# Two fused transformer blocks on one core: three vector products of the modulation moved from the first attention into the recurrence, score products split in three

## The chip, the cores and the metric

The kernel runs on one core of a Trainium2 chip, in one launch. The metric is the device time of one execution in microseconds. TensorE (PE) does the matrix products, VectorE (DVE) and ScalarE (ACT) the elementwise work, GpSimd (POOL) some small vector work and the gathers of expert rows, SyncE (SP) issues most of the transfers. Each engine works through its own list of instructions in order; where one needs another's result, it waits on a semaphore. Matrix products accumulate in PSUM, and all other tiles live in SBUF.

## The reference

Two transformer blocks follow each other on 512 rows of 1024 numbers. The change lies in the first one. Cut to what matters:

```python
def first_block(x, c, ctx, c_ctx, ...):
    mod_x = silu(c) @ w_mod + b_mod                       # 6 parts of 1024
    mod_c = silu(c_ctx) @ w_mod + b_mod
    sh1, sc1, gt1, sh2, sc2, gt2 = split(mod_x, 6)        # parts 0 to 5
    px = split(modulate(rms_norm(x, norm1), sh1, sc1) @ w_in, splits)
    pc = split(modulate(rms_norm(ctx, norm1), csh1, csc1) @ w_in, splits)
    na_x = neighbourhood_attention(q, k, v, k_ctx, v_ctx, na_rpb)   # 8 heads of 64
    hg_x = hgrn2_mixer(px[3:], pc[3:], lb, hg_norm)                 # 4 heads of 128
    x = x + gt1 * (concat([na_x, hg_x]) @ w_out)
    x = x + gt2 * peer_ffn(modulate(rms_norm(x, norm2), sh2, sc2), ...)
    return rms_norm(x, norm_f)
```

`modulate(h, shift, scale)` is `h * (1 + scale) + shift`. Of the modulation, parts 0 and 1 are needed before the projections, part 2 (gt1) behind the output projection, parts 3 and 4 (sh2, sc2) before the expert stage, part 5 (gt2) at the end of the block. In the attention each of 512 queries attends to a window of the grid and to all 256 rows of the context, with a bias for the place in the window.

## The kernel before

The first block runs in this order: modulation parts 0 and 1; the normalised input `hT`, kept in columns; then the recurrence with its projections; then the projections of v, k and q for the attention; the attention; the output projection `w_out`; the routing of the experts; the experts. The order of instructions on each engine is not that of the text: a scheduler takes the program as written and, from its dependencies and from the buffers of the tile pools (a tile of a pool with two buffers must wait until the last but one of the same name has been read), writes an order for each engine.

**Split products.** A product of full precision is made from two tiles in a 32-bit type that PE takes in one pass (`fp32r` in the rows of ACT and DVE): `hi`, a rounded copy made by ACT (L190), and `lo`, the remainder, made by DVE (L191). Three products, hi by hi, hi by lo and lo by hi, add up in PSUM. Every projection is made so: `wload` (L198) loads 256 columns of weights and splits them, `proj_T` and `proj_N` run through eight row tiles with three products each. A plain f32 operand does it in one instruction, which the profile records as two.

**Vector products.** `gemv_T` (L247) makes one part of the modulation, a vector of 1024. The weights come in eight tiles `wg` of 512 KB, two buffers; for each tile `gemv_rows` issues four f32 products that stand beside one another in columns of 32 of the array and add to four groups of rows of one PSUM tile. ACT copies the result into an SBUF tile `row`. Then eight small products with the constant `pick` add the four groups of rows and turn the row into columns of `modT`, with the bias added by DVE. All of one part's columns are made behind its whole row.

**Recurrence** (L385 to L506). Two parts `p`, each of two heads. A part first makes its projections: forget gates in both directions (`F`, from L392), `Qr` (L403), `vn` (L412), `gs` (L421). Then for each head there are a diagonal step and seven levels `k` (from L445): ACT copies halves of the keys into a tile `Kx` (a pool `gla2` with two buffers), PE makes four f32 products of `Kx` and `Q` into a PSUM tile `pA`, DVE merges them and decays keys and queries for the next level. After the levels, PE turns the keys (`kn`), makes the states, the output `pO`, and turns the normalised result `yn` (L506) into a half of `yT`. The scheduler puts the projections of the next part, or those of the attention, between the levels.

**Attention** (L538 to L611). Four pairs of heads `hp2`, each with four blocks of 128 queries. The score products `pS<-kT,qT` are f32 products on 64 rows of the array, one head of the pair on the upper and the other on the lower half: 256 or 384 columns for the window, 256 for the context. DVE adds the bias `nab` and takes the maximum (L578), ACT takes the exponential (L580), PE turns the result (L587), ACT or DVE copies it out (`pT`, L589), PE makes the values `pv`. The bias of a head is loaded once per pair, 2304 columns, in three buffers. Behind pair 0, 1 and 2 the text has `gemv_T` for parts 2, 3 and 4, and the scheduler spreads their products over the pairs behind.

Of the kernel before, what the change touches and what calls it, by code (L numbers as in the profile page):

```python
# [18 lines left out]
P = 128  # L19
# [113 lines left out]
NAB = 3  # L133


def program(tc, a, out, tap=None):
# [41 lines left out]
    class Split:  # L178
        def __init__(self, hi, lo):
            self.hi, self.lo = hi, lo  # L180

# [65 lines left out]
    def gemv_T(pl, ps_pool, wname, part, v, slot, bias, tag="pm"):  # L247
        row = pl.tile([P, D], F32, name="row", bufs=1)
        for h2 in range(2):
# [7 lines left out]
            S.copy(row[:, h2 * 512:(h2 + 1) * 512], ps)  # L257
        ps = ps_pool.tile([P, 512], F32, name=tag)[:, :2 * KT].rearrange("p (k o) -> p k o", o=2)
        for kt in range(KT):
            mm(ps[:, kt, :], row[:, kt * P:(kt + 1) * P], pick[:, v:v + 2])  # L260
        V.tensor_add(modT[:, slot, :], ps[:, :, 0], bias)
# [17 lines left out]

    eY = ExitStack()  # L280
    yp = pool(eY, "yT", side="right")
    yT = yp.tile([P, KT, T], F32, name="yT")
# [85 lines left out]
    kT = kvp.tile([P, 4, TC], F32, name="kT")  # L368
# [14 lines left out]

    with ExitStack() as es:
# [5 lines left out]
        pO = pool(es, "pO", 1, PSUM)  # L390
        for p in range(2):
            Fs = [g2.tile([P, 2, TC], F32, name="F") for _ in range(2)]  # L392
            for d in range(2):
                w = wload("w_in", 8 + 2 * d + p)
                for h in range(2):
# [26 lines left out]
            for t in range(NB):  # L422
# [4 lines left out]
                V.tensor_mul(gs[:, t, :], gs[:, t, :], hgnB)  # L427
            for h in range(2):
# [78 lines left out]
                S.copy(yT[:, 4 + p * 2 + h, :], ps)  # L507
# [16 lines left out]
    def kproj(j):  # L524
        w = wload("w_in", 2 + j)
        for m in range(2):
            ps = pm.tile([P, 512], F32, name="pm")
            proj_T(ps, w, m * P, P, hT, 0, T)
            S.copy(kT[:, 2 * j + m, :T].rearrange("p (b r c) -> p b r c", r=8, c=16), ps.rearrange("p (r b c) -> p b r c", b=4, c=16))
            ps = pm.tile([P, 512], F32, name="pm")  # L530
            proj_T(ps, w, m * P, P, hT, T, L)
            S.copy(kT[:, 2 * j + m, T:], ps[:, :L])
# [5 lines left out]
    with ExitStack() as es:  # L538
        np_ = pool(es, "na")
        n2 = pool(es, "na2", 2)  # L540
        gv = pool(es, "gemv")
        qT = np_.tile([P, 4, T], F32, name="qT")
# [14 lines left out]
        for hp2 in range(4):  # L557
            pv = pV.tile([P, 4, P], F32, name="pv")
            sums = n2.tile([P, 8], F32, name="sums")
            bts = []  # L560
            for hh in range(2):
                bt = n2.tile([P, 2304], F32, name="nab", bufs=NAB)
                DMA.dma_start(bt, a["nab"][2 * hp2 + hh])
                bts.append(bt)
            for qb in (0, 1, 3, 2):
# [3 lines left out]
                b0 = 512 - nw if nk == 3 else 0  # L569
                pss = [pS.tile([P, 1024], F32, name="pS") for _ in range(2)]  # L570
                for c0, c1, x0 in ((b0, b0 + nw, k0 * P), (b0 + nw, b0 + n, T)):
                    for hh in range(2):
                        mm(pss[hh][:, c0:c1], qT[HH[hh], hp2, qb * P:(qb + 1) * P], kT[HH[hh], hp2, x0:x0 + c1 - c0])
                pTs = []
                for hh in range(2):
                    sc = n2.tile([P, 640], F32, name="sc", bufs=4)
                    mx_ = sm.tile([P, 1], F32, name="mx")
                    V.tensor_tensor_reduce(out=sc[:, :n], in0=pss[hh][:, b0:b0 + n], in1=bts[hh][:, off[qb]:off[qb + 1]], scale=1.0, scalar=NEG, op0=OP.add, op1=OP.max, accum_out=mx_)  # L578
# [24 lines left out]
            V.tensor_mul(yT[:, hp2, :].rearrange("p (r b c) -> p b r c", b=4, c=16), pv.rearrange("p b (r c) -> p b r c", c=16),  # L603
# [663 lines left out]
```

## Time and profile before

| | us |
|---|---|
| runs | 2344.86, 2347.52, 2342.06 |
| median of the runs | 2344.86 |
| profiled execution, its own time | 2337.86 |
| span of its profile | 2336.1 |
| PE busy | 2259.9 |
| DVE busy | 1598.4 |
| ACT busy | 980.3 |
| POOL busy | 249.1 |

The busy times are sums over the span; they do not say which engine holds up which stage. The stages that the change touches lie at these places of the span, by the timeline of PE: projections and recurrence of part 0 from 64 us, the level products of part 0 from about 128 us, those of part 1 from about 233 us, the attention from the first score product at 343.6 us to the first product of `w_out` at 467.9 us, the routing from about 521 us.

### The profile page before, as it was taken

The page shows a single profiled execution, that of the slowest core. Times are in us where ns is not written, and L with a number is a line of the kernel's source. Part 1 is how long each engine was busy: PE and PEld are TensorE (multiplying, and loading weights), DVE is VectorE, ACT ScalarE, POOL GpSimd, SP SyncE. Part 2 cuts the span into 40 slices and gives each one's busy share as a digit, 9 for nine tenths or more (in the row PEclk, how much of TensorE's full clock was granted, in tenths as well). Part 3 has the DMA queues.
Part 4 walks back from the last instruction along what each step waited for, and adds up shares of the span by engine and source line. Part 5 has one row for each costly group of instructions (what it writes and reads, how often), then busy time and mean ns, then how long its engine had stood idle before and what let it go on. Part 6 is the DMA issues. An engine that isn't in the chain of part 4 may idle for free. (4 is left out here: it accounts for less than half of the span.)

```text
span 2336.1 us, 34601 instructions
## 1 busy us (share of the span) xinstructions
PE 2259.9 (97%) x13097; PEld 1942.3 (83%) x13097; DVE 1598.4 (68%) x3193; ACT 980.3 (42%) x1828; POOL 249.1 (11%) x159
## 2 busy tenths in 40 slices
PE   7999999998999999999999999999999999989998
PEld 4899986597779999999988888888888786666888
DVE  3674723354359977999689888888898627767344
ACT  4432333333234335877534333333333434446421
POOL 0000000000000000322222222222130000000000
PEclk9999999999999999999999999999999999999999
DMA  7111135625555574999999999999997231120221
GB/s 265 55 57 55 52 118 178 212 101 178 165 196 158 163 258 153 328 320 319 333 360 396 406 347 349 354 362 363 360 380 263 88 103 42 50 86 28 98 92 55
DMA packets 170871, 481.74 MB, mean 206 GB/s; under 512 B 14864, under 2 KB 87952, under 8 KB 153168
## 3 DMA queue, kind: packets, MB, share of 16 engines
q1 hardware_dynamic: 152272, 345.31, 42.7%
q0 software_dynamic: 18432, 134.23, 14.7%
q8 instruction: 103, 1.69, 0.3%
q14 instruction: 64, 0.52, 0.1%
HBM read 431.76 MB, written 46.66 MB: 205 GB/s over the span
## 5 line engine op out<-in xcount | busy, mean ns | idle before, releaser
L191 DVE TENSOR_TENSOR wl<-wr,wh 128x1024 fp32r<-128x1024 f32 (+1 forms) x378 | 456.7, 1211 | 362.3 <-ACT wh L190 359.8
L190 ACT CAST wh<-wr 128x1024 fp32r<-128x1024 f32 (+1 forms) x378 | 394.0, 1043 | 440.4 <-PE pm L176 196.1
L176 PE MATMUL pS<-h2h,wh 128*128 128x384 f32 x1024 | 348.2, 340 | 7.3 <-ACT S L695 7.2
L176 PE MATMUL pS<-h2h,wl 128*128 128x384 f32 x1024 | 346.1, 338 | 0.0
L176 PE MATMUL pS<-h2l,wh 128*128 128x384 f32 x1024 | 345.5, 337 | 0.0
L839 POOL DMA_INDIRECT uv<-in_uv_dram,idx x128 | 225.8, 1764 | 1006.9 <-DVE pacc L846 688.8
L176 PE MATMUL po<-wl,Wh 128*128 128x512 f32 x768 | 299.6, 390 | 1.8 <-DVE wl L191 1.8
L176 PE MATMUL po<-wh,Wl 128*128 128x512 f32 x768 | 299.5, 390 | 0.0
L176 PE MATMUL po<-wh,Wh 128*128 128x512 f32 x768 | 298.9, 389 | 0.0
L176 PEld LDWEIGHTS pS<-h2h,wh 128*128 128x128 f32 x1024 | 193.4, 189 | 11.7 <-ACT S L695 8.7
L176 PEld LDWEIGHTS pS<-h2l,wh 128*128 128x128 f32 x1024 | 193.3, 189 | 2.0 <-issue 0.8
L176 PEld LDWEIGHTS pS<-h2h,wl 128*128 128x128 f32 x1024 | 193.2, 189 | 0.0
L190 ACT CAST Wh<-W 128x384 fp32r<-128x384 f32 x128 | 65.7, 513 | 267.8 <-PE po L176 162.1
L176 PE MATMUL pm<-h2h,wh 128*128 128x512 f32 x432 | 173.5, 402 | 0.2 <-ACT cr L1106 0.2
L176 PE MATMUL pm<-h2h,wl 128*128 128x512 f32 x432 | 171.8, 398 | 0.0
L176 PE MATMUL pm<-h2l,wh 128*128 128x512 f32 x432 | 171.8, 398 | 0.0
L176 PEld LDWEIGHTS po<-wl,Wh 128*128 128x128 f32 x768 | 144.1, 188 | 31.9 <-DVE wl L191 2.6
L176 PEld LDWEIGHTS po<-wh,Wl 128*128 128x128 f32 x768 | 144.1, 188 | 30.3 <-DVE Wl L191 0.3
L176 PEld LDWEIGHTS po<-wh,Wh 128*128 128x128 f32 x768 | 144.2, 188 | 29.2
L846 DVE SCALAR_TENSOR_TENSOR pacc<-uv,dts,pacc 128x1024 f32<-128x1024 f32 x128 | 163.9, 1281 | 1.9
L840 DVE SCALAR_TENSOR_TENSOR pscr<-uv,h 128x1024 f32<-128x1024 f32 x128 | 156.1, 1219 | 1.9 <-DMA uv<-in_uv_dram,idx 0.9
L191 DVE TENSOR_TENSOR Wl<-W,Wh 128x384 fp32r<-128x384 f32 x128 | 70.8, 553 | 47.9 <-ACT Wh L190 47.8
(410 smaller groups left out, 4100.6 us busy)
## 6 DMA issues: line engine op xcount, KB each, us to landing
wr<-in_uT_dram SPq DMA_DIRECT2D x128, 512.0 KB, 6.0
wr<-in_uv_dram SPq DMA_DIRECT2D x128, 512.0 KB, 7.7
gd<-stg SPq DMA_DIRECT2D x12, 2048.0 KB, 12.6
Gt<-gd SPq DMA_DIRECT2D x32, 768.0 KB, 8.4
sd<-S SPq DMA_DIRECT2D x88, 192.0 KB, 3.9
Sr<-sd SPq DMA_DIRECT2D x88, 192.0 KB, 6.8
wr<-in_w_in_dram SPq DMA_DIRECT2D x32, 512.0 KB, 3.6
wg<-in_w_mod_dram SPq DMA_DIRECT2D x32, 512.0 KB, 4.3
```

Of the source, the lines that this page charges most:

```text
L176: PE.matmul(ps, lhs, rhs, start=first, stop=last)
L190: (ehi or S.copy)(hi, src)
L191: (elo or V.tensor_tensor)(lo, src, hi.bitcast(F32), op=OP.subtract)
L839: G.indirect_dma_start(out=uv, out_offset=None, in_=a["uv"], in_offset=bass.IndirectOffsetOnAxis(ap=idx[b][:, j:j + 1], axis=0))
L840: V.scalar_tensor_tensor(scr, uv[:, :D], 1.0, h2g[b], op0=OP.mult, op1=OP.mult, accum_out=dts[b][:, j:j + 1])
L846: V.scalar_tensor_tensor(acc[b], tl[j - j0][:, D:], dts[b][:, j:j + 1], acc[b], op0=OP.mult, op1=OP.add)
```

## The change

**Parts 2, 3 and 4 of the modulation** leave the attention. A generator `gates()` makes them in twelve quarters of 256 columns. One quarter (`gemv_quarters`) is two `wg` tiles with four products each, a copy of the PSUM row by ACT, two products with `pick` and an addition by DVE. The recurrence's text takes a quarter behind each of five pieces of a part's projections, ten in all, and the last two behind the projections of part 1. The weights have a pool of their own with two buffers; the row is a buffer of the recurrence's tile `Kx`.

**The parts that are left in `gemv_T`** (part 5, and those of the second block) are now turned by halves, in a row tile of half the length.

**The score products** are split: `mm3` issues hi by hi, hi by lo and lo by hi, 64 rows each. q is split where it is projected, k for each pair of heads at the pair's start.

**The bias** is loaded per block of queries, at most 640 columns, in six buffers. **`yT`** is two tiles, of which the half for the attention is allotted behind the recurrence.

```diff
-NAB = 3
+NAB = 6
...
+    def mm3(ps, x, y, xi, yi):
+        mm(ps, x.hi[xi], y.hi[yi], True, False)
+        mm(ps, x.hi[xi], y.lo[yi], False, False)
+        mm(ps, x.lo[xi], y.hi[yi], False, True)
...
     def gemv_T(pl, ps_pool, wname, part, v, slot, bias, tag="pm"):
-        row = pl.tile([P, D], F32, name="row", bufs=1)
...
-            S.copy(row[:, h2 * 512:(h2 + 1) * 512], ps)
-        ps = ps_pool.tile([P, 512], F32, name=tag)[:, :2 * KT].rearrange("p (k o) -> p k o", o=2)
-        for kt in range(KT):
-            mm(ps[:, kt, :], row[:, kt * P:(kt + 1) * P], pick[:, v:v + 2])
-        V.tensor_add(modT[:, slot, :], ps[:, :, 0], bias)
+            row = pl.tile([P, 512], F32, name="row", bufs=1)
+            S.copy(row, ps)
+            ps = ps_pool.tile([P, 512], F32, name=tag)[:, :KT].rearrange("p (k o) -> p k o", o=2)
+            for k in range(4):
+                mm(ps[:, k, :], row[:, k * P:(k + 1) * P], pick[:, v:v + 2])
+            V.tensor_add(modT[:, slot, 4 * h2:4 * h2 + 4], ps[:, :, 0], bias[:, 4 * h2:4 * h2 + 4])
...
+    def gemv_quarters(wl, rows, ps_pool, wname, part, v, slot, bias):
+        for hf in range(4):
+            ps = ps_pool.tile([P, 512], F32, name="pm")
+            for k0 in (0, 4):
+                w = wl.tile([P, 4, GW], F32, name="wg", bufs=2)
+                DMA.dma_start(w.rearrange("p k n -> p (k n)"), a[wname][4 * part + hf][:, k0 * GW:(k0 + 4) * GW])
+                gemv_rows(ps[:, :GW], w, k0)
+            row = rows()
+            S.copy(row, ps[:, :GW])
+            ps = ps_pool.tile([P, 512], F32, name="pm")[:, :4].rearrange("p (k o) -> p k o", o=2)
+            for k in range(2):
+                mm(ps[:, k, :], row[:, k * P:(k + 1) * P], pick[:, v:v + 2])
+            V.tensor_add(modT[:, slot, 2 * hf:2 * hf + 2], ps[:, :, 0], bias[:, 2 * hf:2 * hf + 2])
+            yield
...
+    gw = pool(eG, "gw", side="right")
...
+        def gates():
+            for part in (2, 3, 4):
+                yield from gemv_quarters(gw, lambda: g2.tile([P, T], F32, name="Kx")[:, :GW], pm, "w_mod", part, 0, part, bmT[:, part * 8:part * 8 + 8])
+
+        unit = gates()
         for p in range(2):
             Fs = [g2.tile([P, 2, TC], F32, name="F") for _ in range(2)]
             for d in range(2):
...
+                next(unit)
             w = wload("w_in", 6 + p)
...
+            next(unit)
             vn = gp.tile([P, 6, GW], F32, name="vn")
...
+            next(unit)
             hgnB = gp.tile([P, GW], F32, name="hgnB")
...
+            next(unit)
+            if p:
+                for _ in unit:
+                    pass
             for h in range(2):
                 F_, Qr = Fs[h], Qrs[h]
...
-                S.mul(qT[:, 2 * j + m, :].rearrange("p (b r c) -> p b r c", r=8, c=16), ps.rearrange("p (r b c) -> p b r c", b=4, c=16), 0.125)
+                pr = ps.rearrange("p (r b c) -> p b r c", b=4, c=16)
+                q_ = n2.tile([P, 640], F32, name="sc", bufs=4)[:, :T]
+                S.mul(q_.rearrange("p (b r c) -> p b r c", r=8, c=16), pr, 0.125)
+                split(q_, qT.hi[:, 2 * j + m, :], qT.lo[:, 2 * j + m, :])
...
-            bts = []
-            for hh in range(2):
-                bt = n2.tile([P, 2304], F32, name="nab", bufs=NAB)
-                DMA.dma_start(bt, a["nab"][2 * hp2 + hh])
-                bts.append(bt)
+            kT = Split(n2.tile([P, TC], F32R, name="kTh"), n2.tile([P, TC], F32R, name="kTl"))
+            split(k32[:, hp2, :], kT.hi, kT.lo)
             for qb in (0, 1, 3, 2):
...
+                bts = []
+                for hh in range(2):
+                    bt = n2.tile([P, 640], F32, name="nab", bufs=NAB)
+                    DMA.dma_start(bt[:, :n], a["nab"][2 * hp2 + hh][:, off[qb]:off[qb + 1]])
+                    bts.append(bt)
...
-                        mm(pss[hh][:, c0:c1], qT[HH[hh], hp2, qb * P:(qb + 1) * P], kT[HH[hh], hp2, x0:x0 + c1 - c0])
+                        mm3(pss[hh][:, c0:c1], qT, kT, (HH[hh], hp2, slice(qb * P, (qb + 1) * P)), (HH[hh], slice(x0, x0 + c1 - c0)))
...
-            if hp2 < 3:
-                part = 2 + hp2
-                gemv_T(gv, pm, "w_mod", part, 0, part, bmT[:, part * 8:part * 8 + 8])
```

How the orders moved is seen at three places, all on PE. In the rows below a product reads `output<-moving or weight tile, other tile`, then the size of the operand and how many follow one another. Between two levels of the second head of part 0 (`pA<-Q,Kx` are a level's products, `pm<-hTh,wh` and its like a projection), before:

```order
L176 MATMUL pA<-Q,Kx 128x128 x4
L176 MATMUL pm<-hTh,wh 128x512
L176 MATMUL pm<-hTl,wh 128x512
L176 MATMUL pm<-hTh,wl 128x512
...
L176 MATMUL pA<-Q,Kx 128x128 x4
```

and now, with the sixth quarter (`pm<-wg,cvec` its eight products, `pm<-pick,Kx` the two that turn its row) around the last levels:

```order
L176 MATMUL pm<-wg,cvec 32x256 x3
L176 MATMUL pA<-Q,Kx 128x128 x4
L176 MATMUL pm<-wg,cvec 32x256 x5
L543 MATMUL tp<-ident,yn 128x128 x4
L176 MATMUL pA<-Q,Kx 128x128 x12
L176 MATMUL pm<-pick,Kx 128x2 x2
L176 MATMUL pm<-hTh,wh 128x512
L176 MATMUL pm<-hTl,wh 128x512
L176 MATMUL pm<-hTh,wl 128x512
L176 MATMUL pA<-Q,Kx 128x128 x4
```

Eight projection products stood between two levels there; now three levels (x12) follow one another, and the projection goes on behind the two `pick` products. The row that these need is copied by ACT, whose order is now there:

```order
L488 COPY Kx<-K 128x8x32 x2
L488 COPY Kx<-K 128x4x64 x2
L293 COPY Kx<-pm 128x256
L514 COPY kn<-pA 128x512
L515 COPY kn<-pA 128x128
```

The copy of the quarter's row (L293) stands behind the copies of the last level (four blocks of 64), so it comes after them.

At the end of part 1's projections (`pm<-wh,hTh` and its like), PE's order before:

```order
L176 MATMUL pm<-wh,hTh 128x256
L176 MATMUL pm<-wl,hTh 128x256
L176 MATMUL pm<-wh,hTl 128x256
L176 MATMUL pA<-Qr,Kx 128x128 x4
L176 MATMUL pA<-Q,Kx 128x128 x4
```

and now:

```order
L176 MATMUL pm<-wh,hTl 128x256
L176 MATMUL pm<-wg,cvec 32x256 x8
L176 MATMUL pm<-pick,Kx 128x2 x2
L176 MATMUL pm<-wg,cvec 32x256 x8
L176 MATMUL pm<-pick,Kx 128x2 x2
L176 MATMUL pm<-wg,cvec 32x256 x8
L176 MATMUL pm<-pick,Kx 128x2 x2
L176 MATMUL pm<-wh,hTh 128x256
L176 MATMUL pm<-wl,hTh 128x256
L176 MATMUL pm<-wh,hTl 128x256
L176 MATMUL pA<-Qr,Kx 128x128 x4
L176 MATMUL pA<-Q,Kx 128x128 x4
```

Quarters ten to twelve stand in a row, with no other product between them.

In the attention (`pS` scores, `tp` turned probabilities, `pv` values), PE's order before:

```order
L587 MATMUL tp<-ident,sc 128x128 x8
L176 MATMUL pS<-kT,qT 128x384
L176 MATMUL pm<-wg,cvec 32x256 x4
L176 MATMUL pv<-pT,vp 64x128 x8
L176 MATMUL pm<-wg,cvec 32x256 x4
L176 MATMUL pS<-kT,qT 128x256 x5
L176 MATMUL pm<-wg,cvec 32x256 x4
L587 MATMUL tp<-ident,sc 128x128 x5
L176 MATMUL pS<-kT,qT 128x256
```

and now:

```order
L633 MATMUL tp<-ident,sc 128x128 x5
L176 MATMUL pv<-pT,vp 64x128
L176 MATMUL pS<-kTh,qTh 128x384
L176 MATMUL pS<-kTl,qTh 128x384
L176 MATMUL pS<-kTh,qTl 128x384
L176 MATMUL pv<-pT,vp 64x128 x9
L633 MATMUL tp<-ident,sc 128x128 x4
L176 MATMUL pS<-kTl,qTh 128x256
L176 MATMUL pS<-kTh,qTl 128x256
```

The groups of four vector products between the attention's products are gone, and each score product is three, one head's three ahead of the other's. In the whole attention the 64 score products stood in 35 runs, 24 of them alone; the 192 of the change stand in 37 runs.

## Rows read from the trace of the kernel before

**Rows 1.** The page, part 1: busy time of each engine, share of the span, instructions.

```profile
PE 2259.9 (97%) x13097; PEld 1942.3 (83%) x13097; DVE 1598.4 (68%) x3193; ACT 980.3 (42%) x1828; POOL 249.1 (11%) x159
```

**Rows 2.** Stretches: us; busy PE, PEld, DVE, ACT, POOL (instructions); PE clock; DMA share; GB/s.

```profile
64.00:128.00 64.00, 64.00 (x431) 59.28 (x431) 37.85 (x61) 23.85 (x35) 0.00 (x0) 1.00 0.20 66
128.00:204.00 76.00, 74.17 (x485) 66.09 (x484) 59.50 (x108) 27.15 (x71) 2.94 (x2) 1.00 0.13 44
344.00:468.00 124.00, 116.53 (x929) 76.19 (x926) 46.99 (x137) 51.82 (x110) 0.00 (x0) 0.99 0.54 185
```

**Rows 3.** Waits of PE, 64 to 343 us: us in total, times, longest.

```profile
PE tp L506 <- DVE yn L503: 3.4, 4, 1.1
```

**Rows 4.** Waits of PE in the attention.

```profile
PE pm L176 <- DMA wg<-in_w_mod_dram: 3.1, 4, 1.0
PE pS L176 <- DVE mx L578: 2.5, 5, 0.9
```

**Rows 5.** Groups of PE in the attention: busy us, mean ns | idle before, releaser.

```profile
L176 PE MATMUL pS<-kT,qT 64*128 64x256 f32 (+1 forms) x128 | 36.2, 444 | 2.6 <-DVE mx L578 2.5
L176 PE MATMUL pm<-wg,cvec 128*32 128x256 f32 x192 | 15.2, 391 | 3.2 <-DMA wg<-in_w_mod_dram 3.1
```

**Rows 6.** Timeline of PE, 399 to 405 us: start, us with the tail, records.

```profile
399.91 0.70 PE L176 MATMUL pS<-kT,qT 64*128 64x256 f32 x2
400.54 0.64 PE L176 MATMUL pm<-wg,cvec 128*32 128x256 f32 x8
401.11 0.76 PE L587 MATMUL tp<-ident,sc 128*128 128x128 f32 x5
...
402.17 0.91 PE L176 MATMUL pS<-kT,qT 64*128 64x384 f32 x2
403.01 1.95 PE L176 MATMUL pm<-pick,row 128*128 128x2 f32 x16
404.88 0.33 PE L176 MATMUL pv<-pT,vp 128*64 128x128 f32 x2
```

**Rows 7.** Timeline of PE, 360.5 to 362.5 us.

```profile
360.55 1.57 PE L176 MATMUL pS<-kT,qT 64*128 64x256 f32 x8
362.08 0.77 PE L587 MATMUL tp<-ident,sc 128*128 128x128 f32 x5
```

**Rows 8.** Timeline of PE, 290.7 to 291.2 us, a projection's split products.

```profile
290.74 0.28 PE L176 MATMUL pm<-wh,hTh 128*128 128x256 f32 x1
290.86 0.28 PE L176 MATMUL pm<-wl,hTh 128*128 128x256 f32 x1
```

**Rows 9.** Timeline of PE, 381 to 383 us, the first vector products in the attention.

```profile
381.95 1.07 PE L176 MATMUL pm<-wg,cvec 128*32 128x256 f32 x16
382.95 0.43 PE L176 MATMUL pv<-pT,vp 128*64 128x128 f32 x2
```

**Rows 10.** The tile wg, 343 to 480 us: ns of one (min, median, max), first to last.

```profile
L176 PE MATMUL pm<-wg,cvec x192: 379/379/405, 381.9 to 459.2; 128*32 128x256 f32 x192
DMA to landing us min/median/max: 3.1/4.3/6.9
```

**Rows 11.** Groups of ACT, 64 to 343 us.

```profile
L417 ACT COPY vn<-pm 128x256 f32<-128x256 f32 x12 | 4.5, 373 | 24.3 <-PE pm L176 24.3
```

**Rows 12.** Timeline of PE, 159 to 178 us, products of two levels.

```profile
170.00 1.05 PE L176 MATMUL pA<-Q,Kx 128*128 128x128 f32 x8
...
175.66 1.13 PE L176 MATMUL pA<-Q,Kx 128*128 128x128 f32 x8
```

**Rows 13.** Stretches behind the output projection, columns as in rows 2.

```profile
521.00:531.00 10.00, 2.66 (x16) 2.43 (x16) 9.55 (x14) 4.60 (x8) 3.32 (x3) 0.75 0.66 208
531.00:541.00 10.00, 9.28 (x44) 8.51 (x43) 4.81 (x10) 3.35 (x6) 0.00 (x0) 0.73 0.59 211
```

**Rows 14.** Groups of PE's weight loads in the attention.

```profile
L176 PEld LDWEIGHTS pS<-kT,qT 64*128 64x128 f32 x128 | 16.5, 185 | 12.4 <-DVE mx L578 5.6 <-issue 5.2 <-DVE pT L589 0.2
```

**Rows 15.** Waits of PE in the attention up to the first vector product, 343.6 to 381.9 us.

```profile
PE pS L176 <- DVE mx L578: 1.1, 2, 0.8
```

More of the change, by code (lines that the diff above doesn't have):

```diff
@@ L278, in to_hT @@
             split(t[:, :n], x.hi[:, kt, off:off + n], x.lo[:, kt, off:off + n], V.tensor_copy, V.tensor_tensor)
+    def gemv_quarters(wl, rows, ps_pool, wname, part, v, slot, bias):
[12 more added lines that the diff above has]
+            yield
     eY = ExitStack()
-    yp = pool(eY, "yT", side="right")
-    yT = yp.tile([P, KT, T], F32, name="yT")
+    yT = [None] * KT
+    ypb = pool(eY, "yTb", side="right").tile([P, 4, T], F32, name="yTb")
+    for c in range(4):
+        yT[4 + c] = ypb[:, c, :]
     class Turns:
@@ L367, in program @@
     kvp = pool(eH, "nakv")
-    kT = kvp.tile([P, 4, TC], F32, name="kT")
+    k32 = kvp.tile([P, 4, TC], F32, name="kT")
     vp = kvp.tile([P, 6, 512], F32, name="vp")
@@ L382, in program @@
     V.tensor_scalar(lb1, lb0, -1.0, 1.0, op0=OP.mult, op1=OP.add)
+    eG = ExitStack()
+    gw = pool(eG, "gw", side="right")
     with ExitStack() as es:
@@ L506, in program @@
                     PE.transpose(ps[:, c * P:(c + 1) * P], yn[:, c, :], ident)
-                S.copy(yT[:, 4 + p * 2 + h, :], ps)
+                S.copy(yT[4 + p * 2 + h], ps)
+    V.scalar_tensor_tensor(modT[:, 4, :], modT[:, 4, :], 1.0, n2T, op0=OP.add, op1=OP.mult)
+    eG.close()
+    ypa = pool(eY, "yTa", side="right").tile([P, 4, T], F32, name="yTa")
+    for c in range(4):
+        yT[c] = ypa[:, c, :]
     def vproj(j):
@@ L528, in kproj @@
             proj_T(ps, w, m * P, P, hT, 0, T)
-            S.copy(kT[:, 2 * j + m, :T].rearrange("p (b r c) -> p b r c", r=8, c=16), ps.rearrange("p (r b c) -> p b r c", b=4, c=16))
+            S.copy(k32[:, 2 * j + m, :T].rearrange("p (b r c) -> p b r c", r=8, c=16), ps.rearrange("p (r b c) -> p b r c", b=4, c=16))
             ps = pm.tile([P, 512], F32, name="pm")
             proj_T(ps, w, m * P, P, hT, T, L)
-            S.copy(kT[:, 2 * j + m, T:], ps[:, :L])
+            S.copy(k32[:, 2 * j + m, T:], ps[:, :L])
     vproj(0)
@@ L540, in program @@
         n2 = pool(es, "na2", 2)
-        gv = pool(es, "gemv")
-        qT = np_.tile([P, 4, T], F32, name="qT")
+        qT = Split(np_.tile([P, 4, T], F32R, name="qTh"), np_.tile([P, 4, T], F32R, name="qTl"))
         def qproj(j):
@@ L577, in program @@
                     mx_ = sm.tile([P, 1], F32, name="mx")
-                    V.tensor_tensor_reduce(out=sc[:, :n], in0=pss[hh][:, b0:b0 + n], in1=bts[hh][:, off[qb]:off[qb + 1]], scale=1.0, scalar=NEG, op0=OP.add, op1=OP.max, accum_out=mx_)
+                    V.tensor_tensor_reduce(out=sc[:, :n], in0=pss[hh][:, b0:b0 + n], in1=bts[hh][:, :n], scale=1.0, scalar=NEG, op0=OP.add, op1=OP.max, accum_out=mx_)
                     V.tensor_scalar_mul(mx_, mx_, -1.0)
@@ L602, in program @@
             S.copy(rn, rs_)
-            V.tensor_mul(yT[:, hp2, :].rearrange("p (r b c) -> p b r c", b=4, c=16), pv.rearrange("p b (r c) -> p b r c", c=16),
+            V.tensor_mul(yT[hp2].rearrange("p (r b c) -> p b r c", b=4, c=16), pv.rearrange("p b (r c) -> p b r c", c=16),
                          rn.rearrange("p (b r c) -> p b r c", b=4, c=16))
@@ L606, in program @@
                 qproj(1)
-            if hp2 < 3:
-                part = 2 + hp2
-                gemv_T(gv, pm, "w_mod", part, 0, part, bmT[:, part * 8:part * 8 + 8])
-        V.scalar_tensor_tensor(modT[:, 4, :], modT[:, 4, :], 1.0, n2T, op0=OP.add, op1=OP.mult)
-    dbg("yT", yT)
     eH.close()
@@ L663, in program @@
         for kt in range(KT):
-            split(yT[:, kt, :], yS.hi[:, kt, :], yS.lo[:, kt, :], S.copy, V.tensor_tensor)
+            split(yT[kt], yS.hi[:, kt, :], yS.lo[:, kt, :], S.copy, V.tensor_tensor)
         for j in range(4):
```

## The prediction

> **What bounds the kernel now.** The page comes first: TensorE (PE) is busy for 97% of the span [rows 1]. That alone does not say whether a stage could take more work, so the table by stages comes next [rows 2]. While the first recurrence and its projections run (64 to 204 us), PE is busy in 64.0 of 64 us and in 74.2 of 76; in the first attention (344 to 468 us) it is busy in 116.5 of 124. VectorE (DVE) and ScalarE (ACT) are busy there for 47 and 52 us of 124. The waits say the same more sharply: from 64 to 343 us PE waits for another engine only four times, 3.4 us in all [rows 3], and in the attention for 3.1 us on the weights of the vector products and 2.5 us on the softmax [rows 4]. So both stages, the one that loses work and the one that gets it, are bound by PE's own queue. Work that moves from one to the other is worth nothing by itself; what counts is what PE pays around it: changes of array shape, waits, and the clock.
>
> **What leaves the attention.** The page's groups count 192 records of the vector product there [rows 5]; a group of eight records (four products, one beside the other in columns of 32) is one step, so there are 24 steps. In the timeline such a step starts at 400.54 and the next work at 401.11 [rows 6]: 0.57 us, with the drain behind it. 24 x 0.57 = 13.7 us. The sixteen records that turn a row into a column start at 403.01 and end with the next start at 404.88: 1.87 us, three times, 5.6 us. The waits for these weights go too: 3.1 us [rows 4]. Together 22.4 us.
>
> **The score products.** A plain f32 product that stands alone costs 0.63 us at 256 columns (399.91 to 400.54) and 0.84 us at 384 (402.17 to 403.01) [rows 6]; in a run it is cheaper: eight records, so four products, take 1.53 us [rows 7], 0.38 us each. In the order of before, 64 products stand in 35 runs, 24 of them alone: two thirds of the alone ones at 0.63, one third at 0.84, 16.8 us, and 40 at about 0.4, 16 us, so 33 us. The change has 192 products with 64 rows; the trace has none in the split type with 64 rows. The nearest row is the split type with 128 rows: one every 0.12 us at 256 columns [rows 8], 0.18 at 384 in proportion. 144 x 0.12 + 48 x 0.18 = 25.9 us, and 37 runs at about 0.2 us for the change of shape (the 0.63 alone against 0.38 in a run gives that) make 33.3 us: no gain if the two heads never overlap. If they always did, half of 25.9 is saved, 13 us. The order issues the three products of one head before those of the other, which is nearer to the first end: I take 3 us gained. The added splits of k and q on ACT and DVE, under 2 us for each of four head pairs, I cost at nothing: both engines are idle more than half of this stage [rows 2]. The bias table in quarters moves the same bytes. The attention thus gives back 22.4 + 3 = 25.4 us.
>
> **What the recurrence pays.** (a) Twelve quarters. Two adjacent steps cost 1.00 us with the drain (381.95 to 382.95) [rows 9], and four transposing records at 1.87 / 16 another 0.47: 1.5 us x 12 = 18 us, all on the path, since PE has no gap there [rows 3]. (b) In nine of the twelve places the order puts the transposing products right behind the vector product. They need the row, which ACT copies from PSUM after the last product has ended: 0.38 us for that end [rows 10], 0.37 us for a copy of this shape [rows 11], some 0.1 us of hand-over, of which 0.3 was counted as drain. 0.55 x 9 = 5 us. (c) The sixth quarter. Its row is a buffer named Kx, which the level loop of the second head takes in turn; ACT's order has the row's copy behind the last level's copies. The projection cannot go on until that row is transposed, and in PE's order three levels now follow each other with nothing between, where each interval held some eight products before. A level's products start at 170.00, those of the next but one at 175.66 [rows 12]: 2.8 us a level, of which the level's own products take some 0.85. Four intervals lose up to 7.8 us of filling; part returns, since the vector products themselves fill some and levels without filling may follow closer. I take 5 us, bounds 2 and 8. (d) Quarters ten to twelve stand in a row in PE's order, and there are two weight buffers, one quarter's worth. The eleventh's first load can start only when the tenth's first step has freed its buffer: 0.6 us for step and tail, then 4.3 us from issue to landing (3.1 to 6.9) [rows 10], about 5 us a quarter against the 2.05 counted under (a) and (b). Twice 2.95 is 6 us; by the shortest landing 3, by the longest 11. (e) The clock. PE was nearly idle from 521 to 531 (2.7 us busy of 10), and the granted clock was 0.75 and then 0.73 of full speed [rows 13]: PE was at the lower level, 1.2 GHz, for about 0.54 of the second stretch, while it had work for 9.3 us. That lost half of 5.4, 2.7 us. Places (c) and (d) are like it, (c) less so: 1.5 times 2.7 is 4 us, between 0 and 8. The recurrence pays 18 + 5 + 5 + 6 + 4 = 38 us, bounds 26 and 54.
>
> **The other vectors.** The four in the routing stage are now turned by halves, through one PSUM buffer: the second half waits for a turn and an addition. Products stand between; I put a quarter of a microsecond on each, 1 us in all, between 0 and 4.
>
> **The sum.** -25.4 + 38 + 1 = +13.6 us on the profiled execution's 2337.9 us (its span is 2336.1). The runs' median is 2344.9, 7.0 us above it, so I forecast 2344.9 + 13.6 = 2358.5 us, written as 2358.
>
> **Rivals.** *Faster:* the quarters slip into the recurrence without PE standing still. For it speaks that most loads can be issued five or more microseconds ahead. Against it: in (c) and (d) it is the order of PE itself that leaves nothing to do. Then (c), (d) and (e) fall away and 23 us are paid: -25.4 + 23 + 1 = -1.4; with the score products midway between their ends (6.5 us gained) it is -5, 2340 us. It decides once the three cost less than 5 us together. Chance 0.17. *No difference:* stalls of some 10 us and a gain of 27 to 30: within 0.2% of before, 2345 us, chance 0.17. *The attention loses its cover:* the vector products stood where PE would have waited for the softmax. PE waits 2.5 us on it now; without filler the chain of bias, exponential, transposes and copies could show. Against it: until 381.9 us the attention runs without any vector product [rows 10], and PE waits 1.1 us for the softmax there [rows 15]. If half of the 22.4 us comes back as waiting, the sum is +25, 2370 us; chance 0.13. *The split products do not do what they are for:* a weight load that cannot run beside the product before it.
>
> A weight load of a score product takes 185 ns [rows 14], and in the recurrence 128-row products of the split type start every 0.12 us [rows 8] although each has its own load, so loads run beside products there. The Trainium skill, TensorE: Matmul & The Clock Gate, under Part 3: Packing small matmuls, says that a load overlaps with a product in flight only where the two use different groups of rows. The three products of a head use the same rows, so by that rule two loads in each triple would be exposed.
>
> By rows that is 64 x 2 x 0.185 = 23.7 us more: +37, 2382 us. The trace's 128-row products speak against it, so its chance is 0.05. The forecast keeps 0.48.
>
> **How the numbers follow.** The measurement can tell some 0.2%, 4.7 us, from no change. The forecast, the lost cover and the exposed loads are slower by more than that: 0.48 + 0.13 + 0.05 = 0.66. No difference has 0.17 and faster 0.17. The range runs from 2338 (the nearer half of the faster case) to 2374 (the lost cover and a little more); the bounds of (c) to (e) and of the score products lie in it unless they all fall to one side.
>
> **What would show it.** In the changed profile the attention, from the first score product to the first product of the output projection, should last about 99 us instead of 124, without any vector product. The recurrence with its projections should be about 38 us longer. PE should wait for ACT at nine transposing places, by about half a microsecond each; for the weights of the last two quarters by about 3 us each; and stand between the levels of the first part's second head. The granted clock should dip in at least one of these two places. I am wrong if the recurrence grows by less than 28 us, if the attention shrinks by over 35 or by under 15, or if the difference arises behind the first attention.

## The result, and the profile after

The changed kernel takes 2380.69 us (median of 4 runs, 2372.26 to 2383.03); the kernel before takes 2346.19 us beside it (4 runs, 2342.06 to 2350.22). The ratio is 1.0144, interval 1.0121 to 1.0167: 34.5 us slower. The forecast had the sign and 13.6 us; its range ended at 2374 us. The profiled execution has a span of 2377.4 us, 41.3 us more than before, and not 34.5, because the execution profiled before lay 8.3 us under the median of its runs and the one profiled after 1.5 us. The page's first part after (row of before: [rows 1]):

```profile
PE 2281.4 (96%) x13161; PEld 1966.1 (83%) x13161; DVE 1606.0 (68%) x3214; ACT 986.2 (41%) x1842; POOL 259.5 (11%) x159
```

By the timeline of PE, the first score product moved from 343.6 to 393.8 us, the first product of the output projection from 467.9 to 503.2 us. So the recurrence with its projections got 50.2 us longer and the attention 14.9 us shorter: 35.3 of the 41.3 us. The other 6 us lie behind the attention, where one profile cannot tell them: from the first product of the output projection to the end it is 1868.2 us before and 1874.2 after, and in the versions below with the same code there it is anything from 1869.7 to 1875.4. The two stretches as rows (columns as in [rows 2]), before:

```profile
64.00:343.60 279.60, 276.22 (x1924) 255.77 (x1923) 161.15 (x274) 94.20 (x202) 5.33 (x4) 1.00 0.21 70
343.60:467.90 124.30, 116.83 (x930) 76.42 (x929) 46.89 (x137) 51.97 (x110) 0.00 (x0) 0.99 0.54 184
```

and after:

```profile
64.00:393.80 329.80, 308.51 (x2168) 274.46 (x2166) 167.12 (x291) 100.20 (x217) 5.33 (x4) 0.96 0.26 86
393.80:503.20 109.40, 100.60 (x753) 78.08 (x752) 48.94 (x138) 51.94 (x109) 0.00 (x0) 0.89 0.40 129
```

The third number from the end is the granted clock. 0.89 of full speed as a mean over 109.4 us, with levels of 1.0 and 0.5, is 109.4 x 0.11 x 2 = 24 us at the lower level; in the recurrence 0.96 of 329.8 us is about 27 us (by single microseconds 27.3). Before, the recurrence had none and the attention 3.4 us.

In the recurrence, PE waits for more than the four `yn` of [rows 3]. Its waits from 64 to 393.8 us:

```profile
PE pm L176 <- ACT Kx L293: 9.3, 12, 2.5
PE pm L176 <- DMA wg<-in_w_mod_dram: 5.2, 4, 2.4
PE pA L176 <- DVE Q L499: 4.0, 3, 1.5
PE tp L543 <- DVE yn L540: 2.8, 4, 1.1
```

The first row is the hand-over to ACT, at all twelve quarters and not at nine. The second and third are the two places that the prediction named. The sixth quarter, between the levels of part 0's second head, in PE's timeline:

```profile
180.82 1.10 PE L543 MATMUL tp<-ident,yn 128*128 128x128 f32 x4 [0.18 <-DVE yn L540]
182.89 1.13 PE L176 MATMUL pA<-Q,Kx 128*128 128x128 f32 x8 [0.97 <-DVE Q L499]
185.56 2.05 PE L176 MATMUL pA<-Q,Kx 128*128 128x128 f32 x8 [1.54 <-DVE Q L499]
189.08 2.05 PE L176 MATMUL pA<-Q,Kx 128*128 128x128 f32 x8 [1.48 <-DVE Q L499]
191.65 1.01 PE L176 MATMUL pm<-pick,Kx 128*128 128x2 f32 x4 [0.52 <-ACT Kx L293]
```

Three levels with nothing between them, 2.7 and 3.5 us apart. The second and third take 2.05 us in place of 1.13: PE has gone to the lower clock (granted 0.50 from 186 us). The last three quarters:

```profile
268.32 0.61 PE L176 MATMUL pm<-pick,Kx 128*128 128x2 f32 x4 [0.68 <-ACT Kx L293]
271.30 1.08 PE L176 MATMUL pm<-wg,cvec 128*32 128x256 f32 x8 [2.37 <-DMA wg<-in_w_mod_dram]
272.55 1.08 PE L176 MATMUL pm<-wg,cvec 128*32 128x256 f32 x8 [0.17 <-DMA wg<-in_w_mod_dram]
274.18 1.01 PE L176 MATMUL pm<-pick,Kx 128*128 128x2 f32 x4 [0.55 <-ACT Kx L293]
276.63 1.08 PE L176 MATMUL pm<-wg,cvec 128*32 128x256 f32 x8 [1.44 <-DMA wg<-in_w_mod_dram]
278.97 1.08 PE L176 MATMUL pm<-wg,cvec 128*32 128x256 f32 x8 [1.26 <-DMA wg<-in_w_mod_dram]
```

PE stands idle for the weights of quarters eleven and twelve, and again the clock is low. A place that the prediction did not have is the first quarter: PE waits 2.48 us for the copy of its row at 75.24 us. ACT's timeline says why:

```profile
71.31 1.28 ACT L386 ACT_TABLE_LOAD   x1
72.60 0.62 ACT L386 ACTIVATE cosT<-cosT 32x512 f32<-32x512 f32 x1
73.25 1.28 ACT L430 ACT_TABLE_LOAD   x1
74.54 0.38 ACT L430 ACTIVATE F<-pm 128x256 f32<-128x256 f32 x1
74.82 0.37 ACT L293 COPY Kx<-pm 128x256 f32<-128x256 f32 x1
```

ACT changes its function table for a piece of the cosines and back again, 1.28 us each, and the row's copy is queued behind both.

In the attention the low stretches are these (columns as before). PE is busy nearly throughout, but behind the fall, with products that take up to twice as long:

```profile
397.00:407.00 10.00, 10.00 (x48) 7.57 (x48) 4.64 (x15) 4.83 (x13) 0.00 (x0) 0.51 0.49 148
417.00:425.00 8.00, 6.96 (x46) 6.03 (x46) 0.96 (x3) 2.08 (x5) 0.00 (x0) 0.57 0.30 107
441.00:449.00 8.00, 8.00 (x41) 5.89 (x41) 3.90 (x12) 3.21 (x7) 0.00 (x0) 0.57 0.70 229
```

The three microseconds ahead of each, at full clock:

```profile
394.00:397.00 3.00, 2.08 (x19) 1.67 (x18) 2.20 (x7) 2.94 (x4) 0.00 (x0) 1.00 0.18 28
414.00:417.00 3.00, 1.99 (x18) 1.59 (x14) 2.57 (x7) 1.83 (x4) 0.00 (x0) 1.00 0.25 66
438.00:441.00 3.00, 1.38 (x15) 1.01 (x11) 2.25 (x7) 2.14 (x7) 0.00 (x0) 1.00 0.00 0
```

Each fall follows a place where PE stood idle, for 0.9 to 1.6 us of the three, mostly waiting for the softmax.

### The profile page after: what moved, and what is told of

It is laid out like the page before. It is cut to its first block, busy times and chain, and to the rows that moved or that the text cites. A ratio compares the mean times of both kernels' runs of the same rounds, so it can differ in the third digit from the quotient of the medians.

```text
span 2377.4 us, 34852 instructions
## 1 busy us (share of the span) xinstructions
PE 2281.4 (96%) x13161; PEld 1966.1 (83%) x13161; DVE 1606.0 (68%) x3214; ACT 986.2 (41%) x1842; POOL 259.5 (11%) x159
## 5 line engine op out<-in xcount | busy, mean ns | idle before, releaser
L880 POOL DMA_INDIRECT uv<-in_uv_dram,idx x128 | 236.2, 1845 | 1000.2 <-DVE pacc L887 677.5
L176 PE MATMUL pG<-Rh,Lq 128*128 128x128 f32 x768 | 101.5, 279 | 1.9 <-ACT Lq L920 1.7
```

The costliest lines, as they stand in the source:

```text
L176: PE.matmul(ps, lhs, rhs, start=first, stop=last)
L880: G.indirect_dma_start(out=uv, out_offset=None, in_=a["uv"], in_offset=bass.IndirectOffsetOnAxis(ap=idx[b][:, j:j + 1], axis=0))
```

## The experiments

**Theories.** A: the move costs what it shares. The row in the levels' buffer Kx makes the stalls, and the clock falls behind them; in the attention the clock falls because of the split score products. B: it falls there because the vector products are gone. C: the quarters' work itself is what the recurrence pays. Times are compared as ratios to the kernel before, timed on the same chip; 0.1% is 2.3 us. Of every run the granted clock is also known, as a mean over the span: (1 - clock) x span is what PE would have saved at most at full speed, since half of the time at the lower level is lost where PE has work. Before it is 0.987 in the median (30 us), after the change 0.9785 (51 us).

**1. The score products plain again** (`mm3` and the splits of q and k undone; quarters stay).

```diff
-                        mm3(pss[hh][:, c0:c1], qT, kT, ...)
+                        mm(pss[hh][:, c0:c1], qT[...], k32[HH[hh], hp2, x0:x0 + c1 - c0])
```

> The change with its score products undone (one plain f32 product each, no splits of q and k); the quarters stay in the recurrence. Theory A (in the attention the clock falls because of the split score products): the attention, 109.4 us with the change and about 25 us of it at the lower clock, has at most 5 us at the lower clock and lasts 124.2 - 22.4 = 102 us; the time is 5 to 8 us below the change's. Theory B (the clock falls because the vector products are gone): 15 us or more at the lower clock remain, the attention lasts 110 us or more, and the time is that of the change or above it. The recurrence should stay at its length in both.

Ratio 1.0099 (1.0074 to 1.0123), 10 us below the change, where theory A had 5 to 8. Its attention:

```profile
393.60:496.70 103.10, 98.83 (x690) 68.39 (x689) 46.04 (x133) 47.60 (x104) 0.00 (x0) 0.95 0.39 122
```

103.1 us, as theory A had it; 10 us at the lower clock, between the two expectations. The first score product stands at 393.6 us, so the recurrence did not move.

**2. Only the score products split**, with the bias in quarters; vector products stay in the attention.

```diff
-NAB = 3
+NAB = 4
...
+                        mm3(pss[hh][:, c0:c1], qT, kT, ...)
```

> The kernel before with the split score products and the bias in quarters (four buffers), the vector products left in the attention. Theory A: 10 us or more of the attention at the lower clock, so it lasts 124.2 - 3 + 5 = 126 us or more, and the time is that of before or up to 6 us above it. Theory B: no more than the 4 us at the lower clock that the kernel before has there, the attention lasts about 121 us, and the time is 3 us below before.

Ratio 1.0034 (1.0016 to 1.0052), 8 us above before, where theory A had up to 6:

```profile
342.10:472.80 130.70, 121.85 (x994) 88.34 (x993) 50.88 (x142) 54.83 (x115) 0.00 (x0) 0.91 0.57 187
```

With all the vector products in place, 24 us of the attention are at the lower clock, against 3.4. Theory B falls: it comes with the split. (The bias per block of queries comes with it here; the change against run 1 and run 6 against run 7 differ by the split alone.)

**3. A row of its own** for the quarters.

```diff
-lambda: g2.tile([P, T], F32, name="Kx")[:, :GW]
+lambda: kvp.tile([P, GW], F32, name="vt", bufs=2)
```

> The change with the quarters' row in a tile that the recurrence does not use (vt, which lies idle until the projection of v), in place of the level loop's Kx. Theory A (the place of the sixth quarter costs its waits between the levels and the fall of the clock behind them): the idle places of PE from 182 to 192 us, 5.5 us in all, and the 10 us at the lower clock there go; the time is 8 to 10 us below the change's. Rival C (the recurrence pays for the work of the quarters and the turn of the row, wherever the row lies): 3 us below it at most.

Ratio 1.0073 (1.0044 to 1.0101): 16.6 us below the change, more than theory A had.

```profile
64.00:379.80 315.80, 304.99 (x2163) 271.08 (x2161) 165.88 (x289) 99.51 (x217) 4.79 (x4) 0.97 0.27 90
```

The recurrence is 14.0 us shorter, the attention 4.2 us, with 14 us at the lower clock there in place of 24. In the recurrence the stall of the sixth quarter is gone, and the last quarters cost less too: with Kx free, the order itself puts level products of part 1 between them:

```profile
258.20 1.07 PE L176 MATMUL pm<-wg,cvec 128*32 128x256 f32 x16
259.20 0.59 PE L176 MATMUL pA<-Q,Kx 128*128 128x128 f32 x2
259.95 0.61 PE L176 MATMUL pm<-pick,vt 128*128 128x2 f32 x4 [0.16 <-ACT vt L293]
261.59 1.26 PE L176 MATMUL pA<-Q,Kx 128*128 128x128 f32 x8 [1.03 <-DVE Q L499]
262.93 2.27 PE L176 MATMUL pm<-wg,cvec 128*32 128x256 f32 x16
```

**4. The last quarters spread**, the row still in Kx: one more behind the first head of each forget gate of part 1.

```diff
-                next(unit)
+                    if p or h:
+                        next(unit)
...
-            if p:
-                for _ in unit:
-                    pass
```

> The change with the last two quarters taken earlier: one more behind the first head of each forget gate of part 1, so that no three stand in a row. Theory A: the idle places of PE from 270 to 281 us, 8 us in all, shrink to three hand-overs of 0.8 us, and the 13 us at the lower clock there go; the time is 9 to 11 us below the change's. Rival C: 3 us below it at most.

Ratio 1.0137 (1.0111 to 1.0163), the change within its interval, where theory A had 9 to 11 us less. The waits for weights are gone, but the earlier quarters now meet more levels of part 0:

```profile
178.00 0.68 PE L176 MATMUL pA<-Q,Kx 128*128 128x128 f32 x4 [2.43 <-DVE Q L497]
...
182.18 2.05 PE L176 MATMUL pA<-Q,Kx 128*128 128x128 f32 x8 [1.06 <-DVE Q L497]
185.72 2.05 PE L176 MATMUL pA<-Q,Kx 128*128 128x128 f32 x8 [1.49 <-DVE Q L497]
```

The stall moved and kept its size: PE waits 8.6 us for `Q` here, against 4.0 for `Q` and 5.2 for weights in the change, and 27 us of the recurrence are at the lower clock in both. With the row in Kx, quarters and levels got in each other's way at both placements that were tried.

**5. Own row and spread** (3 and 4 together).

> The change with the row in the idle tile vt and the last two quarters taken earlier, but the turning products right behind the copy, as in the change; score products split. It stands between the own row alone (16 us above before) and the version with late turning products (1 us above before). If the hand-over to ACT is what the late turning saves (forecast: 0.55 us in nine places, 5 us), the first score product stands at 374 to 376 us and the time is 5 to 8 us above before. If the spreading of the last quarters made the difference, the first score product stands at 369 to 371 us and the time is within 3 us of the version with late turning.

Ratio 1.0046 (1.0026 to 1.0066), 10.8 us above before, where 5 to 8 were expected; the first score product at 374.7 us as expected. The attention has 14 us at the lower clock.

**6. Own row, spread, and the turning products late**: the two products with `pick` are issued with the next quarter.

```diff
+            if due:
+                due.pop()()
+            due.append(lambda row=row, hf=hf: turn(row, hf))
             yield
```

> The change with the row in the idle tile vt, the last two quarters taken earlier, and the two turning products of each quarter issued with the next quarter's products instead of right behind the copy; score products split. Theory A (sharing Kx makes the stalls, and the hand-over to ACT makes the rest): only the work of 18 us is left in the recurrence, so the first score product stands at 362 to 366 us (393.8 with the change, 379.8 with the own row alone), with less than 8 us at the lower clock before it; the attention still has 12 us or more at the lower clock and lasts 105 to 110 us; the time is 0 to 8 us above before. Rival C (the quarters' work itself costs more than 18 us): the first score product at 372 us or later, 10 us or more above before.

Ratio 1.0004 (0.9984 to 1.0024):

```profile
64.00:369.80 305.80, 299.20 (x2166) 268.40 (x2164) 166.56 (x291) 99.85 (x217) 4.79 (x4) 0.99 0.27 93
369.80:470.60 100.80, 92.04 (x753) 71.81 (x752) 48.86 (x137) 51.81 (x109) 0.00 (x0) 0.98 0.43 140
```

The first score product stands 4.9 us earlier than in 5. It is not at 362 to 366 us: the quarters' work costs more than 18 us. The attention has 3.4 us at the lower clock here, where theory A wanted 12. PE's order in the attention is the same, row for row, in the change and in runs 3, 4, 5 and 6, which have 24, 14, 24, 14 and 3 us at the lower clock: how often it falls differs between executions. The twelve executions of run 6 show it too: their mean granted clocks go from 0.981 to 0.991. Run 6 has the idle place that the change has from 394 to 397 us, and the clock stays up there:

```profile
370.00:373.00 3.00, 2.09 (x19) 1.68 (x20) 2.14 (x7) 2.94 (x4) 0.00 (x0) 1.00 0.17 32
```

**7. The same with plain score products.**

> As the run before, and with plain f32 score products. Theory A: the recurrence as there, the attention 100 to 104 us with at most 10 us at the lower clock; the time is from 6 us below before to equal with it. Rival C: 5 us or more above before.

Ratio 0.9982 (0.9965 to 0.9998), 5 us below 6.

```profile
369.60:468.00 98.40, 94.14 (x690) 65.70 (x689) 45.96 (x133) 47.59 (x104) 0.00 (x0) 1.00 0.40 128
```

**8. The two heads' score products in turn.**

```diff
+                    for i, (qs, ks) in enumerate(((qT.hi, kT.hi), (qT.hi, kT.lo), (qT.lo, kT.hi))):
+                        for hh in range(2):
```

> The change with the three score products of both heads written in turn (one of each head after the other) instead of three of one head and then three of the other. If the heads run side by side only when their products alternate, the attention gets 3 us shorter or more; if the order of writing does not matter, it stays at 109 us within 1.5 us. By Theory A the lower clock stays at 15 us or more in the attention in both cases.

Ratio 1.0160 (1.0134 to 1.0186); no gain from the order of writing. The attention is 4.8 us longer than the change's, outside both expectations, and PE is idle in 11.8 us of it.

```profile
395.70:509.90 114.20, 102.43 (x754) 77.53 (x753) 48.84 (x138) 51.53 (x109) 0.00 (x0) 0.88 0.38 124
```

**9. Only the turn by halves**, on the kernel before.

> The kernel before with the vector products' rows turned by halves, as the change has it, and nothing else; here it concerns seven parts, the three in the attention too. The forecast put 1 us (0 to 4) on the four in the routing stage: the stretch from the first product of the output projection to the first score product of the routing (63 us) and the next one to the first product of the dense experts (655 us) together 0 to 4 us longer. Rival: no difference at all, within 1 us.

Ratio 0.9982 (0.9963 to 1.0001): not slower. In the profile the two stretches together are 724.9 us against 718.5, but among the versions with halves they go from 718.6 to 724.9. The 1 us can't be told.

**10. Halves undone in run 7's version.**

> The version with own row, spread quarters, late turning and f32 score products (5 us below before), with the rows of the vector products that are left in the routing stage turned whole, as before. The turn by halves alone was measured 4 us below before. If that gain comes from the routing stage, this version is 3 to 5 us above the one with halves, that is equal with before. If the move of the quarters is what gains, it stays 4 us or more below before.

Ratio 0.9965 (0.9948 to 0.9982). So the halves don't explain run 7's gain; run 9 and this one put their worth at nothing, within some 0.2%.

**11. Run 7's version with every quarter of part 0 one place later.**

```diff
-                    if p or h:
+                    if p or d:
                         next(unit)
```

> The version with own row, spread quarters, late turning and f32 score products (5 us below before), with every quarter of part 0 taken one place later, so that none stands while ACT loads tables for the cosines. If the wait of 2.4 us at 75 us and the 3.4 us at the lower clock behind it come from that place, both go and the first score product moves from 369.6 to 366 us, the time 3 to 4 us below that version. If the place of the first quarter does not matter, another wait of the same size stands elsewhere and the time is the same within 1.5 us.

Ratio 0.9963 (0.9943 to 0.9982), 9 us below before: with run 10 the lowest of the versions that compute the whole. The runs' times can't tell it from run 10, which has the quarters where run 7 has them; the trace can.

```profile
64.00:366.10 302.10, 297.72 (x2168) 267.42 (x2166) 164.15 (x288) 97.68 (x214) 4.80 (x4) 1.00 0.28 94
366.10:469.20 103.10, 98.83 (x690) 68.39 (x689) 46.06 (x133) 47.61 (x104) 0.00 (x0) 0.95 0.39 122
```

The wait at 75 us is gone, and with it the low clock: the first score product stands at 366.1 us, as expected.

**12. One score product of three**, on run 6's version.

> The version with own row, spread quarters, late turning and split scores, of whose three score products two are left out (hi by lo and lo by hi), so that the scores are computed from the rounded halves alone. It does less work on PE. If the clock falls in the attention because PE is loaded less there (Theory A), the stretch has at least as much time at the lower clock as with three products (3.4 us in the profile) or as the change (24 us), and its length falls by less than 10 us of the some 17 that the left-out products take. If the clock does not depend on it, the attention falls from 100.8 us to 84 us with at most 4 us at the lower clock.

Ratio 0.9966 (0.9947 to 0.9986):

```profile
369.30:462.70 93.40, 85.40 (x626) 62.41 (x625) 47.59 (x138) 51.27 (x109) 0.00 (x0) 0.89 0.47 151
```

Two thirds of the score work left out shorten the attention by 7.4 us, and 20.5 us of it are at the lower clock, against 3.4: theory A's side, as far as one profile goes. The runs' median clock, 0.985 against 0.987 in run 6, points the same way.

**The split, counted three times.** The change against run 1, run 2 against before, run 6 against run 7: split minus plain is 0.45%, 0.34% and 0.22%, that is 10.5, 8 and 5 us. The runs' median granted clocks of these pairs are 0.9785 and 0.983, 0.983 and 0.987, 0.987 and 0.9895: by (1 - clock) x span 11, 9.5 and 6 us. As far as the intervals tell (some 0.2% each), the clock accounts for the whole price of the split. In the profiles, the attention with three split products has 24, 24, 14, 24, 27, 14 and 3 us at the lower clock (the change and runs 2, 3, 4, 8, 5, 6), with plain products 3, 10, 0, 0, 10 and 0 (before and runs 1, 7, 9, 11, 10): a mean of 18.5 and one of 4.

**What goes before the falls.** What it is about the split was not tested apart, but the traces show one more difference. PE is idle for 8.8 us of the attention in the change and in run 6 (109.40 - 100.60, 100.80 - 92.04), and for 4.3 us in runs 1, 7 and 11 (103.10 - 98.83, 98.40 - 94.14). The split saves some of PE's work (92.04 us busy in run 6, 94.14 in run 7), and the waiting takes it back: for the softmax's exponential alone 2.6 us, which the plain versions do not show. Of the 21 falls of the clock in the attentions of all profiles, 18 come a few microseconds at most behind 0.9 to 2.5 us of such idling; the other three (two in run 2, one in the kernel before) have at most 0.2 us of it. So the waits are a rival to the split products themselves as the cause of the falls. They are not the whole of it, as run 2 shows, nor does each of them bring a fall, as run 6 shows; no run here tells the two apart.

## Why the prediction was right or wrong

**Right: the bound, and that the move itself is worth next to nothing.** Both stages are bound by PE in the kernel before. What leaves the attention was reckoned at 22.4 us; with plain score products the attention is 98.4 or 103.1 us against 124.2, 21 to 26 us less, and its two lengths differ by 4.7 us where the clock accounts for half of 10 us. The recurrence takes 22.5 us for it (run 11). Runs 7, 10 and 11, with the scores plain and Kx left to the levels, lie 4 to 9 us below before.

**Right per place: (b), the hand-over.** Reckoned 5 us, nine places at 0.55. In the change PE waits for ACT's copy at twelve places: 2.5 us at the first, 0.52 to 0.68 at the others, 9.3 us in all. Turning late gave back 374.7 - 369.8 = 4.9 us (runs 5 and 6), but that this is the forecast's figure is luck: with a row of its own only eight places wait, 1.35 us of the 4.9 come from the first quarter alone (3.56 us of waiting, then 2.21), and up to 1.7 us are the clock (6.8 us at the lower level, then 3.4).

**Too small: (a), the work.** Run 11 has no stall left that belongs to the quarters, and its recurrence is 366.1 - 343.6 = 22.5 us longer: 1.88 us a quarter, not 1.5.

**Missed: the first quarter.** 369.6 - 366.1 = 3.5 us, for two table loads in ACT's queue. In the change the copy of the row stands behind them. In run 7, where the row is turned late, PE waits 2.2 us at the same place for ACT to read `F` out of PSUM, behind the same two loads, and 3.4 us at the lower clock follow. The prediction costed the copy by its duration [rows 11] and did not look at ACT's queue at that place.

**(c) and (d), the stalls: right places and sizes, the cause of one wrong.** Reckoned 5 + 6 = 11 us; in the change PE waits 4.0 us between the levels and 5.2 us for weights. The prediction took (c) for a matter of Kx and (d) for one of two weight buffers and a row of three quarters. Runs 3 and 4 show that Kx makes most of both: with the quarters spread nothing is gained while they share it; with an own row, the order fills the gap by itself. Taking both stalls away gave back 14.0 (own row) + 5.1 (spread as well, 379.8 - 374.7) = 19.1 us, of which up to 10 us are the clock (27.3 us at the lower level, then 6.8).

The five steps (a, the first quarter, b, the spread, the own row), 22.5 + 3.5 + 4.9 + 5.1 + 14.0 = 50.0 us, add up to the 50.2 read off the traces because they are differences of one row of readings; what is measured is how the 50.2 divide.

**Wrong: the clock.** The step that failed is (e): 4 us, between 0 and 8, for the recurrence, and no term at all for the attention. In the change 27.3 us of the recurrence are at the lower level and 23.9 of the attention, 3.4 us there before; half of these is up to 13.7 and 10.3 us, 24 us together. Without this the recurrence would have paid 36.5 us (forecast without (e): 34) and the attention given back 25.1 (forecast: 25.4), so +11.4 us where the forecast without its clock term has +9.6. The attention gave back 14.9 us, under the 15 that the prediction itself named as a sign of being wrong. The runs' clocks say the same: up to 51 - 30 = 21 us of the 34.5 are the clock. The method of (e) was to scale one idle stretch by 1.5; the clock fell behind shorter waits too, of 0.9 to 1.6 us in the attention.

**The score products.** "I take 3 us gained", between 0 and 13, was right in size at equal clock. With half of the time at the lower clock taken off, the attention is 97.5 us in the change against 98.0 in run 1, 99.1 in run 6 against 98.4 in run 7, and 118.7 in run 2 against 122.6 before: nothing gained in two pairs, 4 us in the third. What they cost is the clock, 5 to 10 us over the pairs. The trace before had a hint that the prediction did not use: the clock's only fall between 64 and 468 us stands in the attention, from 434 us, with PE idle in 0.2 of the 7 us before it.

**Two sums of the prediction that do not come out.** Its bounds for the recurrence, 26 and 54, should be 28 and 50 by the bounds of its terms, which puts the measured 50.2 at their end. And the rival of no difference, with 10 us of stalls and 27 to 30 us gained, comes to 4 to 7 us above before by the prediction's own terms, and not to 0.

**The rivals.** The one of exposed weight loads gave 2382 us, which is close to the time, but not its mechanism. Three products of one head (one call of `mm3`) follow one another like this at full clock, with the load of the second:

```profile
396.18 0.28 PE L176 MATMUL pS<-kTh,qTh 64*128 64x256 f32 x1
396.18 0.18 PEld L176 LDWEIGHTS pS<-kTl,qTh 64*128 64x128 f32 x1
396.30 0.28 PE L176 MATMUL pS<-kTl,qTh 64*128 64x256 f32 x1
396.42 0.28 PE L176 MATMUL pS<-kTh,qTl 64*128 64x256 f32 x1
```

They are 0.12 us apart, each with a load of its own and on the same 64 rows, and the second one's load runs beside the first product: no load of some 185 ns [rows 14] is exposed. The rule of the Trainium skill, TensorE: Matmul & The Clock Gate, Part 3: Packing small matmuls, that a load overlaps only with products on other rows, does not hold for these. The lost cover: PE's waits on the softmax rose from 2.5 us [rows 4] to about 5 (2.4 for the maximum, 2.6 for the exponential), a small part of the 11 us that this rival had as waiting. But all three falls of the clock in the attention come right behind such waits (0.8 us and 0.9 us for the maximum, ended at 395.56 and 415.15 us, 1.6 us for the exponential, ended at 440.40 us); how much of the clock's price belongs to this rival stays open.

## What to carry to other kernels

Work moved into a busy stage must not take its buffers from that stage's innermost loop: one borrowed tile tied two sequences to each other, cost 14 us, and placing the work elsewhere (run 4) did not cure it. Copy such a row into a tile that lies idle, and issue what reads it one step later. And give the clock a term of its own also where PE waits for a microsecond at a time only: three products of the split type in place of one of plain f32 saved 0 to 4 us at equal clock and lost more than that by it, 5 to 10 us net.

## What was not expected of the hardware

The granted clock fell to its lower level in a stage where PE was busy for more than 90% of the time. The 10.00 of 10 us from 397 us do not say that it fell while PE was busy: ahead of that fall PE was busy in 2.08 of 3 us, and idle places of 0.9 to 1.6 us stand ahead of the other two as well. In run 2 it fell twice with PE busy in 3.91 and 4.00 of the 4 us before. And it fell in one execution for 24 us and in another, with the same products of the attention in the same order, for 3.4 us. So the time of such a stretch varies from run to run, and one profile of it tells little: run 6's executions reach from 2342.27 to 2354.87 us. Whether the split products lower the clock by themselves or by the waits that come with them was not settled here; run 12 only shows that fewer of them do not keep it up.
